# A final one-tile batch with pieces of its own, and one-tile exps in two parts

## The chip, the cores and the metric

The kernel runs on one core of one Trainium2 chip. The time is device microseconds of one execution. The kernel before took 336.56 us in the median of three runs (335.83 to 337.37). The execution that was profiled took 335.54 us, of which the span from the first to the last instruction is 333.7 us.

## The reference

32 sequences of at most 512 rows, each with its own length, go through multi-head self-attention with 8 heads of 64 columns. Rows past a sequence's length stay zero.

```
for b in range(batch):
    x_b = x[b, :lengths[b]]
    q, k, v = split(x_b @ w_qkv, 3)            # 512 -> 3 * 512
    q, k, v = [heads of 64 columns, (8, seq_len, 64)]
    scores = (q @ k.T) / sqrt(64)
    attn = exp(scores - max) ; attn /= sum(attn) + 1e-8
    output[b, :lengths[b]] = concat_heads(attn @ v)
```

The lengths are drawn between 64 and 511. In the draw used here the six shortest are 134, 119, 101, 86, 79 and 75.

## The kernel before

**Tiling.** The batches are ranked by length, longest first, and run in pairs (ranks 0 and 1, 2 and 3, and so on). The longer of the two sets the pair's class: a number of rows N from `CLASSES` (multiples of 32, and 340), with T = ceil(N / 128) tiles of 128 rows. In this draw the last pairs have 134 and 119 rows (class 160, two tiles), 101 and 86 (class 128, one tile), and 79 and 75 (class 96, one tile). For each class the program holds straight-line code for two halves, `h` = 0 and 1, one for each batch of a pair.

**A half is software-pipelined.** The half of batch r, with `g = 1 - h`, computes the attention of batch r, and the projections of batch r + 1 and their first scores. With one tile (`T == 1` in `half`, line 691) TensorE's order is: 16 products for the next batch's queries into bank `a0`, 16 for its keys into `a1`, 8 products of exps and values for this batch (`attnv`, line 548), 4 products for the next batch's values (`vwhole`, line 470), 8 score products for the next batch (`scores`, line 306 for the instruction, called at the end of `half`).

VectorE copies `a0` to `qkT` (line 412), takes the reciprocals of the eight sums (line 615), multiplies all eight heads with them and with the row mask in one instruction (line 640), and copies the values to `v_aug` (line 481). ScalarE copies `a1` (line 411), does the exps of all eight heads in one instruction (line 348), and issues the store of the batch (`act_store`, line 832; the DMA itself at line 844), for which it loads the batch's index first (line 1305). The exps are written to `ep`, the ninth element of each head in `v_aug` is the row mask, so that the product also gives the sums.

**Waits.** Each PSUM bank has a semaphore `full` (TensorE to the engine that empties it) and `free` (back). `acquire` makes TensorE wait until a bank is free; `close` puts the `full` on the last product of a group and hangs further signals (`pr.signals`) on the products before it. The exps' `free` is also what the product of exps and values waits for. The normalized output `onat[h]` is guarded by `s_of` (written) and `s_od` (stored).

**Blocks and branches.** `graph` (line 1155) lays the code of each class in blocks: `first` (half 0), then either `again` (half 1, when the next pair has the same class) or `last` (half 1, when it has another), then `tail`, which goes on to the next class. For classes of one tile the `again` blocks lie behind all classes, and `first` ends with a branch (line 1267) that goes on to `last` or away to `again`:

```
bye = name == "act" and T == 1
...
if T == 1:
    br = e.br_cmp(cur, k, out_, label(k, "again"), "IS_NE")
```

ScalarE alone has another block: `mid` (line 1275) looks whether any batch follows, and if none does it goes to `bye`, also behind all classes, where the store is issued ahead of the exp. TensorE and VectorE run the ordinary `last` block for the final batch too: they compute projections, values and scores of a batch that does not exist, from whatever the buffers hold.

**The end.** SyncE (queue SP) transposes, loads and stores for the longer batches; GpSimd (POOL) casts and places rows. After its loops SyncE waits for ScalarE's end (`s_fin`), for the landing of the last stores (line 1642), and then all engines meet in barriers.

Of the kernel before, what the change touches and what calls it, by code (L numbers as in the profile page):

```python
# [11 lines left out]
ALU = mybir.AluOpType  # L12
# [140 lines left out]
def kernel(  # L153
# [118 lines left out]
    for b in halves_av:  # L272
        for g in ("act", "dve"):
            full[(b, g)] = sem(f"f_{b}_{g}")
    free = {b: sem(f"e_{b}") for b in banks + halves_av + ("x0",)}
    area = {
        "a0": pa[:, 0], "a1": pa[:, 1],
        "v0": pav[:, 0:MAXS], "v1": pav[:, MAXS : 2 * MAXS],
# [29 lines left out]
    def scores(pr, slot, h, i, kts, T, N):  # L308

        b = f"s{slot}"  # L310
        qk_h = qkT[h]
        if T == 1:
            def po(par, i, kt):
                return psc[:, slot, par, P * i : P * i + N]

            items = [(j, 0) for j in range(NPAIR)]
            src = psc[:, slot].rearrange("p a (i n) -> p a i n", n=P)[:, :, :, 0:N]
            dst = ep[:, :, :, 0, 0:N].rearrange("p i a n -> p a i n")
        elif T == 2:
            def po(par, i, kt):  # L320
                return psc[:, slot, par, 256 * kt : 256 * kt + N]

            items = [(i, 0), (i, 1)]
            src = psc[:, slot].rearrange("p a (t n) -> p a t n", n=256)[:, :, :, 0:N]
            dst = ep[:, i, :, 0:2, 0:N]
        else:
            def po(par, i, kt):
                return psc[:, slot, par, 0:N]

            items = [(i, kts)]  # L330
            src = psc[:, slot, :, 0:N]
            dst = ep[:, i, :, kts, 0:N]
        mms = []
        for j, kt in items:
            for par in range(2):
                rq = HD * par
                mms.append(
                    mm(
                        po(par, j, kt),
                        qk_h[rq : rq + HD, 2 * j + 1, kt * P : (kt + 1) * P],  # L340
                        qk_h[rq : rq + HD, 2 * j, 0:N],
                        True,
                        True,
                    )
                )
        group(
            pr, b, "act", mms,
            lambda e: e.activation(out=dst, in_=src, func=AF.Exp, scale=scale),  # L348
        )
        pr.pair[b] = i  # L350

    def scores_dense(pr, h, i, N, T):
# [195 lines left out]
    def attnv(pr, h, i, T, late=False, b=None, qts=None):  # L548

        for s_ in ("s0", "s1"):  # L550
            if pr.pair[s_] == i or T == 1 and pr.pair[s_] is not None:
                acquire(pr, s_)
        for v in halves_av if b is None else (b,):
            acquire(pr, v)
        va = v_aug[h]
        if b is not None:
            jobs = [(2 * 74 * k, i, qt) for k, qt in enumerate(qts)]
        elif T == 1:
            jobs = [(74 * 2 * j, j, 0) for j in range(NPAIR)]
        elif T == 4:  # L560
            jobs = [(256 * qt, i, qt) for qt in range(T)]
        else:
            jobs = [(74 * (4 * qt + 2 * (i % 2)), i, qt) for qt in range(T)]
# [19 lines left out]
        if b is not None:  # L583
            n = len(qts)
            res = into[:, 0 : 2 * 74 * n].rearrange("p (t a d) -> p t a d", a=2, d=74)
            dst = on[:, i // 2, qts[0] : qts[0] + n, P * (i % 2) : P * (i % 2 + 1)]
            dst = dst.rearrange("p t (a d) -> p t a d", d=HD)
            sh, fin = [n, 2], i % 2 == 1 and T - 1 in qts
        elif T == 4:
            res = pav.rearrange("p (j n) -> p j n", n=256)[:, :, 0 : 2 * (HD + 1)]  # L590
            res = res.rearrange("p j (a d) -> p j a d", d=HD + 1)
            dst = on[:, i // 2, :, P * (i % 2) : P * (i % 2 + 1)]
            dst = dst.rearrange("p t (a d) -> p t a d", d=HD)
            sh, fin = [NT, 2], i % 2 == 1
        else:
            sh, fin = [2, 4] if T == 1 else [T, 4], True
            res = pav[:, 0 : 74 * sh[0] * 4].rearrange("p (b j d) -> p b j d", j=4, d=74)
            if T == 1:
                dst = on[:, :, 0, :].rearrange("p b (j d) -> p b j d", d=HD)
            else:  # L600
                dst = on[:, i // 2, 0:T, :].rearrange("p t (a d) -> p t a d", d=HD)
        r0 = 2 * qts[0] if b is not None else 0
        rv = rcp[:, i, r0 : r0 + sh[0] * sh[1]].rearrange("p (j a) -> p j a", a=sh[1])
        num, den = res[..., 0:HD], res[..., HD]
# [4 lines left out]

        def recip():  # L610
            opens = i % 2 == 0 and (b is None or 0 in qts)
            for j in (0, 1) if T == 1 else (i // 2,) if not each or opens else ():
                pr.take("dve", s_od[h][j], 16)
            pr.take("dve", full[(name, "dve")])
            pr.add("dve", lambda e: e.reciprocal(out=rv, in_=den).then_inc(s_r, 1))  # L615

        def mult():
            pr.take("dve", s_r)

            if T == 1:  # L620
                cuts = [(slice(0, 2), 0)]
            elif b is not None:
                whole = [] if h else [k for k, t in enumerate(qts) if t < T - 1]
                cuts = [(slice(0, len(whole)), None)] if whole else []
                cuts += [(slice(k, k + 1), t) for k, t in enumerate(qts) if k not in whole]
            elif h == 0:
                cuts = [(slice(0, T - 1), None), (slice(T - 1, T), T - 1)]
            else:
                cuts = [(slice(t, t + 1), t) for t in range(T)]

            def fn(e):
                for w, t in cuts:
                    ops = dict(
                        out=dst[:, w], in0=num[:, w],
                        in1=rv[:, w].unsqueeze(3).broadcast_to(list(num[:, w].shape)),
                    )
                    if t is None:
                        ins = e.tensor_tensor(op=ALU.mult, **ops)
                    else:
                        ins = e.scalar_tensor_tensor(  # L640
                            scalar=now[0][:, 1, t : t + 1], op0=ALU.mult, op1=ALU.mult, **ops
                        )
                if fin:
                    ins.then_inc(s_of[h][i // 2], 1)
                if back is not None:
                    if fin:
                        ins = e.memset(small, 0.0)
                    ins.then_inc(free[back], 1)

            pr.add("dve", fn)  # L650
            if back is not None:
                pr.busy[back] = True

        todo = {"R": recip, "X": mult}
        if not late:
            for fn in todo.values():
                fn()
        return todo

    def acquire_carry(pr, mms):  # L660
        carry, pr.signals = pr.signals, []
# [31 lines left out]
    def half(pr, h, T, N, W, st, last=False):  # L693
# [2 lines left out]
        tiles = -(-W // P)  # L696
        pr.signals += [s_vf[g]] if T == 1 else [s_xtf[h], s_vf[g]]

        def start_proj():
            if not st["x"]:  # L700
                st["x"] = True
                pr.take("pe", s_xt[g], 64)
                pr.signals.append(s_x16f[g])

        if T == 1:
            start_proj()
            qk(pr, "a0", g, [(i, 0) for i in range(NPAIR)], W, P)
            qk(pr, "a1", g, [(i, 1) for i in range(NPAIR)], W, P, "act")
            attnv(pr, h, 0, 1)
            vwhole(pr, g)  # L710
            read_class(pr, h)
            for b in ("a0", "a1"):
                acquire(pr, b)
            pr.signals.append(s_xtf[g])
            pr.take("pe", s_on[g])
            if last:
                act_store(pr, h, 0, T)
            scores(pr, h, g, 0, 0, 1, W)
            if not last:
                act_store(pr, h, 0, T)  # L720
            return
        per = T if T >= 3 else 1
        ahead = tiles if T >= 3 else 1
# [138 lines left out]
    def make_body(N, W, last=False):  # L862
# [4 lines left out]
        for h in range(2):  # L867
            st["x"] = False
            pr.add("dve", lambda e: set_now(e))
            half(pr, h, T, N, (N, W)[h], st, last and h == 1)  # L870
            pr.add("dve", lambda e: e.reg_add(rank_reg[0], rank_reg[0], 1))
            if h == 0:
                pr.second = {g: len(ops) for g, ops in pr.ops.items()}
        assert (st["slot"], st["bank"], len(st["banks"])) == (0, 0, len(area))
        ops = [op for op in pr.ops["pe"] if isinstance(op, Matmuls)]
        ops[-1].carry([free[b] for b in banks + halves_av if not pr.busy[b]])
# [281 lines left out]
    def graph(e, name, opening=None, before=None):  # L1158
# [86 lines left out]
        for k, N in enumerate(CLASSES):  # L1245
# [15 lines left out]
                stay[N].run_part(e, 0, cut(k) or stay[N].second[name], entry)  # L1261
            else:
                stay[N].run_half(name, e, 0)
            bye = name == "act" and T == 1
            out_ = label(k, "mid" if bye else "last")
            if T == 1:
                br = e.br_cmp(cur, k, out_, label(k, "again"), "IS_NE")
            else:
                br = e.br_cmp(cur, k, label(k, "again"), out_, "IS_EQ")
                again(k)  # L1270
# [19 lines left out]
        for k, N in enumerate(CLASSES):  # L1290
            if N <= P:
                again(k)
            if name == "act" and N <= P:
                open_(label(k, "bye"))
                final[N].run_half(name, e, 1)
                e.br(label(n, "end"))
# [578 lines left out]
```

## Time and profile before

| What | Value |
|---|---|
| median of three runs | 336.56 us |
| the profiled execution | 335.54 us |
| its span | 333.7 us |
| mean granted TensorE clock | 0.994 |
| TensorE products, busy | 321.6 us (96%) |
| ScalarE, busy | 247.0 us (74%) |
| VectorE, busy | 204.8 us (61%) |
| GpSimd, busy | 67.6 us (20%) |
| `ACT ep L348`, 193 exps | 157.0 us |
| `out_dram<-onat`, ACTq, 256 KB, 16 stores | 3.4 us to landing |

How to read it: busy time of an engine counts its instructions of work; branches, register and semaphore instructions and the issuing of DMAs are not in it. In a row of the timeline stand the start in microseconds from the span's start, the duration, the engine, the source line, the operation, what it writes and reads, its shape and count, and in brackets the idle time before it with what ended it. PE is a TensorE product, PEld its weight load, ACT is ScalarE, DVE VectorE, a trailing q means the engine's sequencer or queue. The four one-tile halves are the last 20 us of the span, out of 333.7; in the rest nothing of the code is touched.

### The profile page before, as it was taken

The page shows a single profiled execution, that of the slowest core. Times are in us where ns is not written, and L with a number is a line of the kernel's source. Part 1 is how long each engine was busy: PE and PEld are TensorE (multiplying, and loading weights), DVE is VectorE, ACT ScalarE, POOL GpSimd, SP SyncE. Part 2 cuts the span into 40 slices and gives each one's busy share as a digit, 9 for nine tenths or more (in the row PEclk, how much of TensorE's full clock was granted, in tenths as well). Part 3 has the DMA queues.
Part 4 walks back from the last instruction along what each step waited for, and adds up shares of the span by engine and source line. Part 5 has one row for each costly group of instructions (what it writes and reads, how often), then busy time and mean ns, then how long its engine had stood idle before and what let it go on. Part 6 is the DMA issues. An engine that isn't in the chain of part 4 may idle for free. (4 is left out here: it accounts for less than half of the span.)

```text
span 333.7 us, 12386 instructions
## 1 busy us (share of the span) xinstructions
PE 321.6 (96%) x4388; PEld 208.0 (62%) x4389; DVE 204.8 (61%) x578; ACT 247.0 (74%) x357; POOL 67.6 (20%) x126
## 2 busy tenths in 40 slices
PE   6999999999999999999999999999999999999991
PEld 2665544455565656566566666677677777787760
DVE  3676567556475575566566557665745656767671
ACT  4568787788889878878978887887677676666641
POOL 3634020201011210220220222022111231131340
PEclk9999999999999999999999999999999999999997
DMA  6976799956654986985787987998688667768742
GB/s 211 346 175 217 194 387 223 324 152 219 142 197 126 333 264 172 293 305 163 238 313 215 226 285 257 204 240 227 197 148 206 206 182 161 177 195 140 202 140 71
DMA packets 83234, 72.35 MB, mean 217 GB/s; under 512 B 41612, under 2 KB 64140, under 8 KB 83156
## 3 DMA queue, kind: packets, MB, share of 16 engines
q1 hardware_dynamic: 71300, 59.84, 65.7%
q10 hardware_dynamic: 11856, 11.54, 10.1%
q8 instruction: 40, 0.66, 0.8%
q14 instruction: 38, 0.31, 0.3%
HBM read 25.32 MB, written 36.70 MB: 186 GB/s over the span
## 5 line engine op out<-in xcount | busy, mean ns | idle before, releaser
L348 ACT ACTIVATE ep<-psc 128x704 f16<-128x704 f32 (+7 forms) x193 | 157.0, 860 | 45.0 <-PE psc L306 32.3
L306 PE MATMUL pa<-xT,w_r 128*128 128x224 f16 (+21 forms) x984 | 122.9, 276 | 1.5 <-DVE qkT L412 0.7
L306 PEld LDWEIGHTS pa<-xT,w_r 128*128 128x128 f16 (+1 forms) x984 | 71.8, 97 | 29.6 <-issue 8.8
L306 PE MATMUL psc<-qkT 64*128 64x352 f16 (+17 forms) x700 | 68.2, 287 | 0.8 <-ACT ep L380 0.2
L412 DVE CAST qkT<-pa 128x512 f16<-128x512 f32 (+9 forms) x61 | 35.0, 574 | 44.5 <-PE pa L306 40.5
L306 PE MATMUL pa<-w_r,xT 128*128 128x512 f16 (+4 forms) x332 | 57.9, 330 | 0.0
L306 PE MATMUL pav<-v_aug,ep 128*128 128x65 f16 x1254 | 55.0, 194 | 0.4 <-PEq L61 0.4
L306 PEld LDWEIGHTS pav<-v_aug,ep 128*128 128x128 f16 x1254 | 49.0, 98 | 9.2 <-issue 1.7
L306 PE MATMUL pav<-xT,w_r 64*128 64x352 f16 (+12 forms) x392 | 50.8, 307 | 0.0
L380 ACT ACTIVATE ep<-psc 128x960 f16<-128x960 f32 (+3 forms) x48 | 42.9, 952 | 9.1 <-PE psc L306 6.0
L411 ACT CAST qkT<-pa 128x320 f16<-128x320 f32 (+8 forms) x74 | 34.4, 470 | 18.8 <-PE pa L306 13.6
L640 DVE SCALAR_TENSOR_TENSOR onat<-pav,masks,rcp 128x128 f32<-128x128 f32 (+2 forms) x124 | 44.4, 396 | 5.0 <-DVE rcp L615 1.9
L1713 POOL MEMSET v_aug<- 128x256 f16 x24 | 7.5, 314 | 186.2 <-POOLq L1301 186.2
L306 PEld LDWEIGHTS psc<-qkT 64*128 64x128 f16 x700 | 26.5, 94 | 28.1 <-issue 17.6
L1707 POOL CAST x<-x_nat 128x1536 f16<-128x1536 f32 (+3 forms) x33 | 42.0, 1272 | 7.9 <-POOLq L1301 7.7
L435 DVE TENSOR_TENSOR v_aug<-pa,masks 128x512 f16<-128x512 f32 (+1 forms) x46 | 30.7, 673 | 16.7 <-PE pa L306 16.4
L306 PEld LDWEIGHTS pav<-xT,w_r 64*128 64x128 f16 (+1 forms) x392 | 26.6, 94 | 12.4 <-issue 1.3
L306 PEld LDWEIGHTS pa<-w_r,xT 128*128 128x128 f16 (+2 forms) x332 | 22.7, 98 | 16.6 <-issue 4.1
L306 PE MATMUL pav<-w_r,xT 128*128 128x512 f16 (+3 forms) x124 | 26.9, 350 | 0.0
L615 DVE RECIPROCAL rcp<-pav 128x8 f32<-128x8 f32 (+2 forms) x69 | 13.6, 197 | 19.7 <-PE pav L306 15.1
L306 PEld LDWEIGHTS pa<-v_aug,ep 128*128 128x128 f16 x538 | 19.7, 98 | 7.0 <-issue 2.9
L306 PE MATMUL pa<-v_aug,ep 128*128 128x65 f16 x538 | 22.3, 194 | 0.0
(84 smaller groups left out, 169.8 us busy)
## 6 DMA issues: line engine op xcount, KB each, us to landing
out_dram<-zt SPq DMA_DIRECT2D x16, 768.0 KB, 6.0
x_nat<-in_x_dram SPq DMA_DIRECT2D x12, 512.0 KB
x_nat<-in_x_dram SPq DMA_DIRECT2D x5, 1024.0 KB
out_dram<-onat ACTq DMA_DIRECT2D x12, 384.0 KB, 5.2
out_dram<-onat SPq DMA_DIRECT2D x12, 384.0 KB, 4.5
x_nat<-in_x_dram SPq DMA_DIRECT2D x17, 256.0 KB, 5.7
out_dram<-onat ACTq DMA_DIRECT2D x16, 256.0 KB, 3.4
x_nat<-in_x_dram SPq DMA_DIRECT2D x4, 768.0 KB
```

What stands on the lines that cost most here:

```text
L306: return lambda e: e.matmul(o, lhsT, rhs, start=start, stop=stop)
L348: lambda e: e.activation(out=dst, in_=src, func=AF.Exp, scale=scale),
L380: lambda e, par=par, b=b: e.activation(out=ep[:, i, par, 0:T, 0:N], in_=psc_f[:, par, 0 : T * N].rearrange("p (t n) -> p t n", n=N), func= ...
L411: return lambda e: e.copy(out=dst, in_=src)
L412: return lambda e: e.tensor_copy(out=dst, in_=src)
L435: return lambda e: e.tensor_tensor(out=v_aug[h][:, t, lo // HD : lo // HD + n, 0:HD], in0=area[b][:, 0:w].rearrange("p (a d) -> p a d", d=HD),
L615: pr.add("dve", lambda e: e.reciprocal(out=rv, in_=den).then_inc(s_r, 1))
L640: ins = e.scalar_tensor_tensor(scalar=now[0][:, 1, t : t + 1], op0=ALU.mult, op1=ALU.mult, **ops)
L1707: e.tensor_copy(out=x16[h][:, 0:T, :], in_=x_nat[h][:, 0:T, :]).then_inc(s_xc[h], 1)
L1713: e.memset(v_aug[h][:, T - 1, NPAIR:NH, 0:HD], 0.0)
```

## The change

Four things are changed, all for classes of one tile.

- **Exps in two parts.** `scores` no longer closes the group with one exp for eight heads but with two, of four heads each. The first raises a new semaphore `s_part`, the second the bank's `free`.
- **`attn_one` in place of `attnv`.** Of the eight products of exps and values, four wait for the first part and four for the second. In the ordinary half the normalization stays one reciprocal and one multiply over all heads.
- **The final batch's own pieces.** With `last`, `half` does nothing but the attention of this batch: no projections, values, scores or exps for a next one. The two groups of four heads go to two PSUM banks, with a reciprocal and a multiply each, and ScalarE stores each half of the columns with a DMA of its own (`store`, the form of line 1309 before, with one tile) instead of one DMA for both. The signals that release POOL and SP are hung on the first products.
- **The blocks.** TensorE and VectorE have `mid` and `bye` as ScalarE has. The branch at the end of `first` is now the same for all classes: `again` follows `first` directly, and `mid` and `last` lie behind it; `bye` lies behind all classes.

```diff
+    s_part = [sem(f"s_part{h}") for h in range(2)]
@@ scores
+            parts = [slice(0, 2), slice(2, NPAIR)]
...
-        group(
-            pr, b, "act", mms,
-            lambda e: e.activation(out=dst, in_=src, func=AF.Exp, scale=scale),
-        )
+        def exp(e, part=None):
+            at = (slice(None), slice(None), part) if part else slice(None)
+            return e.activation(out=dst[at], in_=src[at], func=AF.Exp, scale=scale)
+
+        if T == 1:
+            acquire(pr, b)
+            close(pr, b, "act", mms, False)
+            pr.take("act", full[(b, "act")])
+            pr.add("act", lambda e: exp(e, parts[0]).then_inc(s_part[slot], 1))
+            pr.add("act", lambda e: exp(e, parts[1]).then_inc(free[b], 1))
+            pr.busy[b] = True
+        else:
+            group(pr, b, "act", mms, exp)
@@ new
+    def attn_one(pr, h, ends):
+
+        for v in (f"s{h}",) + halves_av:
+            acquire(pr, v)
+        pr.take("pe", s_part[1 - h])
+        size = MAXS if ends else 74 * 4
+        res = pav[:, 0 : 2 * size].rearrange("p (b n) -> p b n", b=2)[:, :, 0 : 74 * 4]
+        res = res.rearrange("p b (j d) -> p b j d", d=74)[:, :, :, 0 : HD + 1]
+        mms = [
+            mm(res[:, k // 4, k % 4, :], ep[:, k // 2, k % 2, 0, 0:P], v_aug[h][:, 0, k, :],
+               True, True)
+            for k in range(NH)
+        ]
+        av = full[("av", "dve")]
+        if ends:
+            close(pr, "av", "dve", mms[:NPAIR], False)
+        else:
+            acquire_carry(pr, mms[:NPAIR])
+        acquire(pr, f"s{1 - h}")
+        close(pr, "av", "dve", mms[NPAIR:], False)
+        dst = onat[h][:, :, 0, :].rearrange("p b (j d) -> p b j d", d=HD)
+        rv = rcp[:, 0, 0:NH].rearrange("p (b j) -> p b j", j=4)
+        for j in range(2):
+            pr.take("dve", s_od[h][j], 16)
+
+        def recip(w):
+            pr.take("dve", av)
+            pr.add("dve", lambda e: e.reciprocal(out=rv[:, w], in_=res[:, w, :, HD]).then_inc(
+                s_r, 1))
+
+        def mult(w, done):
+            pr.take("dve", s_r)
+            num = res[:, w, :, 0:HD]
+            pr.add("dve", lambda e: e.scalar_tensor_tensor(
+                out=dst[:, w], in0=num, scalar=now[0][:, 1, 0:1],
+                in1=rv[:, w].unsqueeze(3).broadcast_to(list(num.shape)),
+                op0=ALU.mult, op1=ALU.mult,
+            ).then_inc(s_of[h][done], 1))
+
+        parts = (slice(0, 1), slice(1, 2)) if ends else (slice(0, 2),)
+        for w in parts:
+            recip(w)
+        for done, w in enumerate(parts):
+            mult(w, done)
@@ half
+        if last:
+            pr.signals += [s_x16f[g], s_xtf[g]]
+            attn_one(pr, h, True)
+            pr.add("act", act_index)
+            for j in range(2):
+                pr.take("act", s_of[h][j])
+                pr.add("act", lambda e, j=j: store(e, regs_act["bi"], h, j, T))
+            return
...
-            attnv(pr, h, 0, 1)
+            attn_one(pr, h, False)
...
-            if last:
-                act_store(pr, h, 0, T)
             scores(pr, h, g, 0, 0, 1, W)
-            if not last:
-                act_store(pr, h, 0, T)
+            act_store(pr, h, 0, T)
@@ graph
-            bye = name == "act" and T == 1
+            bye = T == 1
...
-                br = e.br_cmp(cur, k, out_, label(k, "again"), "IS_NE")
+                br = e.br_cmp(cur, k, label(k, "again"), out_, "IS_EQ")
...
-            if name == "act" and N <= P:
+            if N <= P:
                 open_(label(k, "bye"))
```

More of the change, by code (lines that the diff above doesn't have):

```diff
@@ L550, in attnv @@
         for s_ in ("s0", "s1"):
-            if pr.pair[s_] == i or T == 1 and pr.pair[s_] is not None:
+            if pr.pair[s_] == i:
                 acquire(pr, s_)
@@ L557, in attnv @@
             jobs = [(2 * 74 * k, i, qt) for k, qt in enumerate(qts)]
-        elif T == 1:
-            jobs = [(74 * 2 * j, j, 0) for j in range(NPAIR)]
         elif T == 4:
@@ L595, in attnv @@
         else:
-            sh, fin = [2, 4] if T == 1 else [T, 4], True
+            sh, fin = [T, 4], True
             res = pav[:, 0 : 74 * sh[0] * 4].rearrange("p (b j d) -> p b j d", j=4, d=74)
[L598 to L601, printed above, removed]
+            dst = on[:, i // 2, 0:T, :].rearrange("p t (a d) -> p t a d", d=HD)
         r0 = 2 * qts[0] if b is not None else 0
@@ L611, in recip @@
             opens = i % 2 == 0 and (b is None or 0 in qts)
-            for j in (0, 1) if T == 1 else (i // 2,) if not each or opens else ():
+            for j in (i // 2,) if not each or opens else ():
                 pr.take("dve", s_od[h][j], 16)
@@ L618, in mult @@
             pr.take("dve", s_r)
-            if T == 1:
-                cuts = [(slice(0, 2), 0)]
-            elif b is not None:
+            if b is not None:
                 whole = [] if h else [k for k, t in enumerate(qts) if t < T - 1]
@@ L873, in make_body @@
                 pr.second = {g: len(ops) for g, ops in pr.ops.items()}
+        if last:
+            return pr
         assert (st["slot"], st["bank"], len(st["banks"])) == (0, 0, len(area))
```

## The prediction

> **What bounds the kernel now.** The page's head and its chain of waits come first, because the chain tells which end of the kernel is being cut.
>
> ```profile
> span 333.7 us, 12386 instructions
> ACT ep L348 0%
> L1642 SPq EVENT_SEMAPHORE  x1: 2591/2591/2591, 328.5 to 328.5; - x1
> SPq L1642 <- DMA out_dram<-onat: 2.6, 1, 2.6
> ```
>
> The chain names only the last exp on ScalarE, which is a shred of the span: the work that really ends last does not show as busy time. The other two rows are of line 1642, SyncE's wait for the landed stores, and of SyncE's own waits: from 328.5 it waits 2.59 us for a store of `onat`, to 331.06, and the remaining 2.6 us of the span are the closing barriers. So the end is: last product, its normalization, its store, its landing. The timeline of the last two halves shows that path:
>
> ```profile
> 320.50 0.34 PE L306 MATMUL psc<-qkT 64*128 64x96 f16 x8
> 322.54 0.32 PEld L306 LDWEIGHTS pav<-v_aug,ep 128*128 128x128 f16 x8 [0.28 <-issue]
> 322.83 1.02 PE L306 MATMUL psc<-w_r,xT 128*128 128x512 f16 x4
> 323.78 0.34 PE L306 MATMUL psc<-qkT 64*128 64x96 f16 x8
> 324.06 1.11 PE L306 MATMUL pa<-xT,w_r 128*128 128x64 f16 x32
> 324.10 0.75 DVE L481 TENSOR_SCALAR v_aug<-psc,masks 128x512 f16<-128x512 f32 x1
> 324.27 0.81 ACT L348 ACTIVATE ep<-psc 128x768 f16<-128x768 f32 x1 [0.95 <-ACTq L61]
> 325.35 0.32 PEld L306 LDWEIGHTS pav<-v_aug,ep 128*128 128x128 f16 x8 [0.30 <-issue]
> 325.38 0.42 PE L306 MATMUL pav<-v_aug,ep 128*128 128x65 f16 x8 [0.21 <-PEq L61]
> 325.64 1.02 PE L306 MATMUL psc<-w_r,xT 128*128 128x512 f16 x4
> 325.95 0.21 DVE L615 RECIPROCAL rcp<-pav 128x8 f32<-128x8 f32 x1 [0.54 <-DVEq L61]
> 326.23 0.37 ACT L411 CAST qkT<-pa 128x256 f16<-128x256 f32 x1 [1.15 <-ACTq L61]
> 326.41 0.75 DVE L640 SCALAR_TENSOR_TENSOR onat<-pav,masks,rcp 128x512 f32<-128x512 f32 x1 [0.25 <-DVEq L61]
> 327.40 0.56 ACTq L844 DMA_DIRECT2D out_dram<-onat  x1
> 328.18 0.60 ACT L348 ACTIVATE ep<-psc 128x512 f16<-128x512 f32 x1 [1.58 <-ACTq L61]
> ```
>
> Read: exp 324.27 to 325.08, product 325.35 to 325.80, reciprocal 325.95 to 326.16, multiply 326.41 to 327.16, store issued at 327.40. The projections of 64 columns at 324.06, the value projection at 325.64 and the exp at 328.18 belong to a batch that does not exist. The projections end at 325.17 and the product cannot start until the exp's 325.08, so they cost the path nearly nothing.
>
> The last leg, 327.40 to 331.04, is the longest. The stores of line 844 (the first row pair without the final one, the second the final one alone), and the DMA queues in three stretches (328.1 to 328.6, 328.6 to 329.5, 329.55 to 331.1; the last column is a share of 16 engines over the stretch):
>
> ```profile
> L844 ACTq DMA_DIRECT2D out_dram<-onat x3: 556/557/688, 318.7 to 325.0; - x3
> DMA to landing us min/median/max: 2.5/2.5/2.6
> ...
> L844 ACTq DMA_DIRECT2D out_dram<-onat x1: 557/557/557, 327.4 to 327.4; - x1
> DMA to landing us min/median/max: 3.6/3.6/3.6
> ...
> q8 instruction: 1, 0.02, 16.9%
> q10 hardware_dynamic: 255, 0.25, 77.4%
> q10 hardware_dynamic: 16, 0.02, 4.2%
> ```
>
> Three equal stores landed in 2.5 us; the final one took 3.6. A packet of instructions starts before 328.6 and holds one DMA engine for 0.169 x 16 x 0.5 = 1.35 us; 255 of the store's 272 packets then move within 0.9 us, and 16 trickle out after 329.55. One engine's share of the store stood behind the instructions: about 1.1 us of the end.
>
> **Part 1: the final batch's own pieces.** Removed: 32 projections, 4 value projections, 8 scores on TensorE, two evacuations on VectorE, a cast and an exp on ScalarE, all of them beside or behind the path above: worth 0, except the cast that stands ahead of the final index load in ScalarE's order (about 0.1 us of waiting and dispatch). POOL's and SP's pieces for the missing batch stay; they are released by the product's first three matmuls instead of the projections, some 0.9 us later, and SP was idle from before 328.5, so that costs 0 with cover down to 329.
>
> What is added is a way there. The final pieces now lie in a block of their own behind the others on TensorE and VectorE as already on ScalarE, and the "mid" and "last" blocks lie behind the "again" block. The branch rows:
>
> ```profile
> L1269 PEldq COMPARE_BRANCH  x14: 66/340/367, 42.0 to 308.1; - x14
> L1269 DVEq COMPARE_BRANCH  x14: 43/63/63, 43.9 to 309.4; - x14
> L1228 PEldq COMPARE_BRANCH  x13: 75/86/528, 23.6 to 326.9; - x13
> L1267 PEldq COMPARE_BRANCH  x2: 66/66/66, 317.1 to 323.5; - x2
> L1267 DVEq COMPARE_BRANCH  x2: 43/43/43, 318.4 to 324.7; - x2
> L1275 ACTq COMPARE_BRANCH  x2: 34/42/50, 319.5 to 325.7; - x2
> ```
>
> Line 1267, this branch today, falls through in 66 ns on TensorE. Line 1269, the same branch of larger classes, jumps over an "again" block at 340 ns, and the dearest jump of the kernel, to the end, is 528. TensorE meets the branch at 323.5 and needs the final product's weights at about 324.9: 0.34 + 0.53 is covered, up to 1.4 us. VectorE meets it at 324.7 and needs its reciprocal at 325.5: its two jumps have no row; between 0.1 (two times 63 ns) and 1.0 (two of TensorE's dearest) I take 0.4, nearest to the VectorE rows, which is hidden. ScalarE makes its far jump today: branch at 325.7, next instruction by 326.23, half a microsecond; the nearer jump adds about 0.1.
>
> [...]
>
> **Part 2: exps in two parts, four halves.** By form:
>
> ```profile
> L348 ACT ACTIVATE ep<-psc x5: 597/810/1023, 314.6 to 328.2; 128x1024 f16<-128x1024 f32 x2, 128x768 f16<-128x768 f32 x2, 128x512 f16<-128x512 f32 x1
> 300.60 1.30 ACT L348 ACTIVATE ep<-psc 128x640 f16<-128x640 f32 x2
> ```
>
> 512, 768 and 1024 columns take 597, 810 and 1023 ns: 0.83 ns a column and 0.17 fixed. Two parts of 384 are 0.49 each; two neighbours of 640 took 0.65 each where the fit gives 0.70, so the pair is some 0.93: its end is 0.12 later than the whole, its first half 0.3 earlier. For the earlier three halves the product waits for projections, so the price is on TensorE: one wait more (the two waits ahead of 325.35 held it 0.27 after the exp, so 0.05 to 0.15 each), and one jump at 317.1 that grows from 66 to 340 ns. In the half at 322.54 the bubble of 0.28 is exposed already. I take +0.15 for the start of the last exp (bounds -0.1, the first four products going early, and +0.5, three waits at 0.15 bare).
>
> **Part 3: two halves of product, normalization and store.** From an exp at 324.42: second part done 325.35, its weights 0.2 later (bounds 0.1 and 0.27), four products instead of eight end at 325.87 (0.19 for one, three more at 0.03); before it was 325.80. The first four are through by then. Second reciprocal 0.15 later, as now, 326.02 to 326.23. The multiplies and the store's other form:
>
> ```profile
> L640 DVE SCALAR_TENSOR_TENSOR onat<-pav,masks,rcp x3: 475/484/751, 314.0 to 317.0; 128x256 f32<-128x256 f32 x2, 128x512 f32<-128x512 f32 x1
> L1309 ACTq DMA_DIRECT2D out_dram<-onat x1: 379/379/379, 314.1 to 314.1; - x1
> L1309 SPq DMA_DIRECT2D out_dram<-onat x1: 413/413/413, 318.0 to 318.0; - x1
> DMA to landing us min/median/max: 2.1/2.2/2.3
> L1305 ACTq TENSOR_LOAD <-idx x32: 274/287/689, 42.1 to 326.3; - x32
> ```
>
> Two multiplies at 0.48 follow without the 0.25 gap, since their waits are met: 326.75 and 327.2, against 327.16. ScalarE's index load begins at 326.3 today; with 0.15 from upstream, 0.1 for the nearer jump, 0.1 less for the cast and 0.5 for the load it is through at about 327.0, so the first store goes at 327.2; it takes 0.38 to issue, and with the 0.24 from data to issue seen today (327.16 to 327.40) the second goes at 327.8, 0.4 later than today's only one. Its bytes are half. A store of this form and 256 KB lands in 2.1 to 2.3; halving the 0.9 us of movement makes 1.85 (bounds 1.6 and 2.3). It lands at 329.65, against 331.04: about -1.4 us, and -1.3 after rounding the unseen VectorE jump in.
>
> [...]
>
> The gain is thus not in the arithmetic (0.1 either way) but in the landing: 1.1 because TensorE is done by 325.6 and fetches its closing instructions before the stores move, 0.4 for fewer bytes and 0.3 for the shorter issue form, less 0.4 for issuing in series.
>
> **The rivals.** First, the second store stands behind an instruction packet as the single one does: for it, that a packet followed each engine's late jumps and the change adds jumps; against, that these fall near 325 to 327 and the packets of the second store near 329. Price 1.1 to 1.35: 336.5, no change.
>
> [...]
>
> [...]
>
> Fourth, a larger gain: the final index load at its 0.29 and VectorE's first multiply at 326.5 let the stores go at 326.75 and 327.2, landing at 328.95: -2.1, 334.5.
>
> **How the numbers follow.** The profiled execution took 335.54, 1.02 under the median of 336.56; a shift of -1.3 makes it 334.2, and the median 335.3, which I predict. The forecast (gain 0.7 to 1.7) has 0.58, the larger gain 0.16, the first rival 0.12, the second 0.08, the third 0.06. Half a per cent, 1.7 us, is about what a measurement of this kernel can tell from no change: faster than that is most of the larger gain and the forecast's edge with the spread of the runs, 0.22; slower only the third, 0.05; between them 0.73. The range from 334.2 to 336.7 takes in the larger gain and the first rival.
>
> **What would show it.** Right: SyncE's wait at its landed-store line ends near 329.7; two stores on ScalarE's queue some 0.6 apart with landings under 2.3; two exps of about 0.49 in the last four halves; no 64-column projections at the end. Wrong: a landing over 3, a gap of over 1.4 on TensorE between the last scores and the first product, or scores of the last halves that start over 0.5 later than 320.50 and 323.78.

## The result, and the profile after

The changed kernel takes 338.77 us in the median of five runs (338.65 to 339.18), against 336.56 (335.83 to 337.37) before: a ratio of 1.0072, interval 1.005 to 1.0095. It is slower by about 2.2 us, where 335.3 was forecast.

The profiled execution after took 338.9 us with a span of 337.1, which is 3.4 more than the profiled one before. One microsecond of that is the choice of executions: before's was 1.02 under its median, after's 0.13 over its own. The two traces differ upstream by 1.8 us: the last scores start at 325.55 instead of 323.78, and 1.5 of it is there ahead of the first class, where TensorE's branch of line 1300 (1243 before) starts at 24.9 instead of 23.4. Within the last pair it loses nothing: its two groups of scores lie 3.25 us apart (322.30, 325.55) and lay 3.28 apart before (320.50, 323.78). What the change did is therefore read from the last scores on.

The timeline of the changed kernel from there:

```profile
322.30 0.35 PE L307 MATMUL psc<-qkT 64*128 64x96 f16 x8 [0.17 <-PEq L61]
...
325.55 0.34 PE L307 MATMUL psc<-qkT 64*128 64x96 f16 x8
...
326.04 0.87 ACT L350 ACTIVATE ep<-psc 128x384 f16<-128x384 f32 x2 [0.76 <-ACTq L61]
...
329.83 0.47 PEld L307 LDWEIGHTS pav<-v_aug,ep 128*128 128x128 f16 x8 [4.08 <-issue]
329.86 0.60 PE L307 MATMUL pav<-v_aug,ep 128*128 128x65 f16 x8 [3.96 <-PEq L61]
330.27 0.51 DVE L691 RECIPROCAL rcp<-pav 128x4 f32<-128x4 f32 x2 [3.65 <-PE pav L307]
330.75 0.88 DVE L697 SCALAR_TENSOR_TENSOR onat<-pav,masks,rcp 128x256 f32<-128x256 f32 x2
331.50 0.98 ACTq L1366 DMA_DIRECT2D out_dram<-onat  x2
```

The two exps end at 326.91 and the products start at 329.86. Nothing that they need is late: their weight load waited 4.08 us for "issue", and the reciprocal's 3.65 is only that wait passed on. What TensorE's sequencer did in it stands in its branches. The groups of three source lines (duration minimum/median/maximum, then the first and the last start) are line 1324, the branch at the end of `first`, line 1332, the one from `mid` to the final block, and line 1353, the jump from there to the end:

```profile
L1324 PEldq COMPARE_BRANCH  x2: 225/473/721, 318.9 to 325.4; - x2
L1332 PEldq COMPARE_BRANCH  x2: 68/1707/3346, 319.1 to 326.2; - x2
L1332 DVEq COMPARE_BRANCH  x2: 43/52/62, 320.3 to 326.7; - x2
L1332 ACTq COMPARE_BRANCH  x2: 40/42/45, 321.4 to 327.6; - x2
L1353 PEldq COMPARE_BRANCH  x1: 2927/2927/2927, 330.1 to 330.1; - x1
```

On TensorE one branch, the jump to the final block at 326.2, took 3346 ns. The same line fell through in 68 ns seven microseconds earlier, and costs VectorE and ScalarE 62 and 45 ns. In the middle of that jump the DMA queues of the stretch from 326.8 to 328.2 show one packet of instructions on q8:

```profile
q8 instruction: 1, 0.02, 5.6%
```

It holds one of 16 engines for 0.056 x 16 x 1.4 = 1.25 us. The jump is thus longer than its packet, which starts at 326.86 in the trace: about 0.7 us before it and 1.4 behind it.

Part of the loss comes back at the stores. First the groups of line 1366, the two stores, with the time from issue to landing, and of line 1699, where SyncE has waited for them:

```profile
L1366 ACTq DMA_DIRECT2D out_dram<-onat x2: 351/363/375, 331.5 to 332.1; - x2
...
DMA to landing us min/median/max: 1.7/2.2/2.6
L1699 SPq EVENT_SEMAPHORE  x1: 28/28/28, 334.7 to 334.7; - x1
```

Then the DMA queues between 333.1 and 334.0, and between 333.85 and 334.8 (queue, kind, packets, MB, share of 16 engines):

```profile
q8 instruction: 1, 0.02, 10.6%
q14 instruction: 2, 0.02, 7.9%
...
q10 hardware_dynamic: 9, 0.01, 2.5%
```

The first store landed in 1.7 us. The second took 2.6: packets of instructions (two of q14, one of q8) moved at the same time, and the store's last nine packets trickle out after 333.85. That these nine stood behind such a packet on one engine is a reading; the view does not name the engines.

The leg from the last scores to the landing in both traces (us):

| Leg | before | after | difference |
|---|---|---|---|
| last scores to first final product | 1.60 | 4.31 | +2.71 |
| first final product to the last store's issue | 2.02 | 2.26 | +0.24 |
| issue of the last store to its landing | 3.64 | 2.61 | -1.03 |
| sum | 7.26 | 9.18 | +1.92 |
| landing to the end of the span | 2.69 | 2.37 | -0.32 |

The net of +1.6 lies near the 2.2 of the medians; the other 0.6 I could not place. The +0.24 is partly the clock: the eight products took 0.60 us at a granted clock of 0.50 (it is 0.50 from 327.9 on), where they took 0.42 at 1.00 before. With the jump announced (below), at nearly the same wait (3.91 us against 3.96), they took 0.44, and the last slice of `PEclk` on that page is 6. In the changed kernel's page that slice is 5 where all others are 9:

```profile
PEclk9999999999999999999999999999999999999995
```

### The profile page after: what moved, and what is told of

Read it like the earlier page. It is cut to its first block, busy times and chain, and to the rows that moved or that the text cites. A ratio compares the mean times of both kernels' runs of the same rounds, so it can differ in the third digit from the quotient of the medians.

```text
span 337.1 us, 12292 instructions
## 1 busy us (share of the span) xinstructions
PE 321.3 (95%) x4344; PEld 207.7 (62%) x4345; DVE 204.7 (61%) x578; ACT 246.4 (73%) x359; POOL 67.4 (20%) x126
## 5 line engine op out<-in xcount | busy, mean ns | idle before, releaser
L350 ACT ACTIVATE ep<-psc 128x704 f16<-128x704 f32 (+8 forms) x196 | 156.8, 849 | 43.6 <-PE psc L307 32.9
L307 PE MATMUL pa<-xT,w_r 128*128 128x224 f16 (+19 forms) x952 | 121.7, 278 | 1.9 <-DVE qkT L1014 0.9
L307 PEld LDWEIGHTS pa<-xT,w_r 128*128 128x128 f16 (+1 forms) x952 | 70.9, 97 | 29.6 <-issue 8.9
L644 DVE SCALAR_TENSOR_TENSOR onat<-pav,masks,rcp 128x128 f32<-128x128 f32 (+1 forms) x120 | 41.4, 384 | 4.2 <-DVE rcp L621 1.6
L621 DVE RECIPROCAL rcp<-pav 128x8 f32<-128x8 f32 (+2 forms) x65 | 12.7, 196 | 17.5 <-PE pav L307 14.5
```

The lines of the kernel that those rows point to most:

```text
L307: return lambda e: e.matmul(o, lhsT, rhs, start=start, stop=stop)
L350: return e.activation(out=dst[at], in_=src[at], func=AF.Exp, scale=scale)
L644: ins = e.scalar_tensor_tensor(scalar=now[0][:, 1, t : t + 1], op0=ALU.mult, op1=ALU.mult, **ops)
```

## Experiments

Ratios are to the kernel before, measured on the same chip beside each set. The theory (A) is that TensorE's one jump to the far block costs 3 us (3346 ns in the trace) and is the whole loss, because its code is not yet fetched; that reason is an assumption, since the traces show packets of instructions but not what an engine holds. The rivals are the exps in parts, the two stores, and a block that costs its fetch wherever it lies (B in the last set).

**The final block directly behind its branch.** Only the order of the targets is turned, which lays the block of the first-named target behind the branch:

```diff
-                e.br_cmp(cur, n, label(k, "last"), label(k, "bye"), "IS_LT")
+                e.br_cmp(cur, n, label(k, "bye"), label(k, "last"), "IS_EQ")
```

> The changed kernel with one edit: the final block lies directly behind the branch that leads to it, on all engines, instead of behind all classes. Theory A (TensorE's branch to a block that lies far off held it for 3.35 us in the changed kernel's trace, and that is the loss): the branch at that line falls under 0.2 us, the idle time between the last scores and the final product falls from 4.1 us to about 0.9, and the time falls by some 2.7 us to 336 (335.3 to 336.7). Theory B (the loss is in the 1.5 us that the changed kernel's trace is late before the first loop, or in the two stores): the time stays at 338 or above.

Measured: 335.94 us, ratio 0.9959 (0.9935 to 0.9984), so 1.4 us under the kernel before. The groups of the branch, of the jump to the end and of the two stores:

```profile
L1332 PEldq COMPARE_BRANCH  x2: 63/145/227, 319.0 to 326.1; - x2
...
L1353 PEldq COMPARE_BRANCH  x1: 4326/4326/4326, 326.9 to 326.9; - x1
...
L1366 ACTq DMA_DIRECT2D out_dram<-onat x2: 527/853/1179, 328.3 to 329.1; - x2
...
DMA to landing us min/median/max: 3.1/3.3/3.5
```

Its timeline, last scores and first final products:

```profile
325.36 0.35 PE L307 MATMUL psc<-qkT 64*128 64x96 f16 x8
...
326.67 0.48 PE L307 MATMUL pav<-v_aug,ep 128*128 128x65 f16 x8 [0.96 <-PEq L61]
```

Its DMA queues from 326.5 to 332.5:

```profile
q8 instruction: 3, 0.05, 4.6%
q14 instruction: 4, 0.03, 2.1%
```

The 3.35 us are gone: 1.31 from the scores to the products. The dear jump has moved behind the products (line 1353, 4326 ns), where nobody waits for it, but packets of instructions (three of q8, four of q14) now move in the stretch of the stores: each takes 3.1 us or more to land, against 1.7 for the changed kernel's first. From the last scores to the last landing it is 6.77 us, against 7.26 before and 9.18 in the changed kernel.

**A far block for TensorE alone**, in the kernel before; the final batch runs its ordinary pieces there.

```diff
-            bye = name == "act" and T == 1
+            bye = name in ("act", "pe") and T == 1
...
-                final[N].run_half(name, e, 1)
+                (final if name == "act" else leave)[N].run_half(name, e, 1)
```

> The kernel before with one edit: TensorE alone reaches the final batch's unchanged pieces by a jump to a block behind all classes; nothing else is changed. Theory A: the branch takes about 3 us, of which 0.6 are covered by the scores in flight, and the time is 338.9 to 339.8. Theory B: the jump costs at most the 0.5 us of the dearest jump in the trace of before, and the time stays within 336 to 337.

Measured: 346.83 us, ratio 1.0302 (1.0255 to 1.0349): 10 us, three times what was expected. The groups of its branch to the block and of its last branch:

```profile
L1275 PEldq COMPARE_BRANCH  x2: 68/1789/3510, 320.2 to 327.2; - x2
...
L1870 PEldq COMPARE_BRANCH  x2: 179/1793/3407, 0.8 to 340.6; - x2
```

The timeline of its 32 projections in that block:

```profile
330.86 0.69 PE L306 MATMUL pa<-xT,w_r 128*128 128x64 f16 x10 [3.11 <-PEq L61]
333.84 1.35 PE L306 MATMUL pa<-xT,w_r 128*128 128x64 f16 x22 [2.29 <-issue]
```

The last branch of the kernel before, the same line:

```profile
L1870 PEldq COMPARE_BRANCH  x2: 179/242/306, 0.8 to 331.9; - x2
```

The jump alone (3510 ns), without the other parts, does the harm. The trace shows two more stops: the engine stops again after ten projections of the new block, for 2.3 us, and the branch at the very end takes 3407 ns where it took 306 before.

**The exps in two parts alone**: `scores` and `attn_one` of the changed kernel, the final batch as before.

```diff
-        group(pr, b, "act", mms, lambda e: e.activation(...))
+        if T == 1:
+            ...two exps of four heads, s_part and free
-            attnv(pr, h, 0, 1)
+            attn_one(pr, h, False)
```

> The exps in two parts and the product in two groups of four heads in all four one-tile halves, and nothing else: the final batch runs the ordinary block as before, with one store, and the blocks lie as before. Theory A: within 0.4 us of before, 336.2 to 337.0, since the scores of the last halves start no later. Theory B in the form that the parts cost: about 338.

Measured: 336.85 us, ratio 0.9995 (0.997 to 1.002). The parts neither gain nor cost.

**The block near, and the `again` blocks far**, as they were before the change:

```diff
-                br = e.br_cmp(cur, k, label(k, "again"), out_, "IS_EQ")
+                br = e.br_cmp(cur, k, out_, label(k, "again"), "IS_NE")
```

> The final block directly behind its branch, and the block for a further pair of the same class behind all classes again, as before the change, so that neither branch of the last pairs jumps. Theory A: TensorE's first branch falls from 0.72 to under 0.1 us too; the time is 335.0 to 336.3, 0.2 to 0.5 below the run with the near final block alone, and under the kernel before. Theory B: 338.

Measured: 339.3 us, ratio 1.0051 (1.0022 to 1.008); a miss. The stores land early, 5.87 us after the last scores instead of 7.26, but the program's last branch is on the path:

```profile
L1927 PEldq COMPARE_BRANCH  x2: 179/1974/3770, 0.8 to 331.6; - x2
```

It jumps over the `again` blocks after all stores have landed, in 3770 ns, and no work hides it. The kernel before has the same three blocks in the same place and pays 306 ns there. The length of the jump does not decide alone; what else does is not shown here.

**The jump announced.** In the changed kernel the outcome of the branch is announced in the entry of `first`, 3.4 us ahead:

```diff
+                if T == 1:
+                    end_hint.append(hint(cur, ALU.is_lt, n))
...
+                for at in end_hint:
+                    br.branch_hint(at)
```

> The changed kernel as it is, blocks where they are, with one instruction pair more on TensorE: behind the first 16 projections of a one-tile pair it announces whether the branch to the final block will be taken. Theory A (the branch waited for its instructions to be fetched): the branch falls from 3.35 us to under 0.6, the final product follows the last scores within 1.3 us, and the time is 335.0 to 336.3, 0.3 to 0.7% under the kernel before. Theory C (what counts is the position of the code and not the moment of the fetch): the branch stays at about 3 us and the time at 338.5.

Measured: 338.11 us, ratio 1.0015 (0.9989 to 1.0041). The groups of its branch and of its two stores:

```profile
L1336 PEldq COMPARE_BRANCH  x2: 68/1569/3070, 319.6 to 326.7; - x2
...
DMA to landing us min/median/max: 1.7/1.7/1.7
```

The branch still took 3070 ns, as theory C has it, and both pages count 41 packets on q8 and 38 on q14: with the announcement no packet more moved. The end is 1.1 us shorter than in the changed kernel (8.06 against 9.18 from scores to landing), 0.9 of it in the landing of the second store (1.7 against 2.6). Why the announcement did nothing is open; that the branch stands right behind another jump is a guess.

**The same announcement in the kernel with TensorE's far block alone.**

> The kernel before with TensorE's jump to the far block for the final batch, and with the same announcement. Its block holds 68 products, and in the run without announcement TensorE stopped a second time inside it, after 10 of them. Theory A: the branch falls from 3.5 us to under 0.6; the second stop either stays (then 342 to 344) or goes too (337 to 338). Theory C: 346 to 347 as without.

Measured: 345.82 us, ratio 1.0225 (1.0185 to 1.0265); the branch took 3630 ns. No help here either. Its 32 projections (the block holds 52 products, not 68) show the second stop again:

```profile
329.15 0.39 PE L306 MATMUL pa<-xT,w_r 128*128 128x64 f16 x8 [3.29 <-PEq L61]
332.44 1.44 PE L306 MATMUL pa<-xT,w_r 128*128 128x64 f16 x24 [2.89 <-issue]
```

It comes after eight products here and came after ten without the announcement, whose instructions push the block a little further on. So the stop seems to belong to a place in the code and not to a number of products.

**The exps whole again**, in the announced kernel (one exp of eight heads, all products behind it):

```diff
-        if T == 1:
-            ...two exps
-        else:
-            group(pr, b, "act", mms, exp)
+        group(pr, b, "act", mms, exp)
```

> As the first run of this set, but the exps of the four one-tile halves are one instruction each again and the eight products wait for it together; the final batch's two halves of normalization and store stay. If the parts are worth nothing (the first part's products wait for the second all the same): within 0.3 us of the first run. If the parts are what brings the final store forward: 0.3 to 0.6 us slower than it.

Measured: 337.6 us, ratio 0.9997 (0.9975 to 1.002), 0.5 us under the announced kernel with intervals that overlap. With the run of the parts alone: the parts are worth nothing that shows.

**One normalization and one store**, in the announced kernel:

```diff
-            attn_one(pr, h, True)
-            ...two stores
+            attn_one(pr, h, False)
+            act_store(pr, h, 0, T)
```

> As the first run of this set, but the final batch is normalized by one reciprocal and one multiply and stored by one DMA of 256 KB, in the form of before. The prediction had 0.4 us for fewer bytes, 0.3 for the shorter issue and minus 0.4 for issuing in series: by it this is 0.2 to 0.5 us slower than the first run, with a landing of about 2.5 us, or 3.6 if a packet of instructions stands ahead of it. If the two stores are no better than one: within 0.2 us, or faster.

Measured: 340.75 us, ratio 1.0095 (1.0062 to 1.0128), 2.6 us over the announced kernel. The group of its last store:

```profile
L896 ACTq DMA_DIRECT2D out_dram<-onat x1: 553/553/553, 331.7 to 331.7; - x1
...
DMA to landing us min/median/max: 2.8/2.8/2.8
```

From scores to landing it is 9.64 against 8.06 us: 1.1 of the 1.6 in the landing (2.8 against 1.7) and 0.35 in a longer gap at the jump of this trace (4.60 against 4.25), which is not the stores' doing. So in this place the two halves are worth more than was thought, about 1.2 us by the traces, though packets of instructions moved beside the one store too (three of q8 and three of q14 between 326 and 336). The medians differ by more; the execution that was profiled here is 2.0 under its median.

**The distance.** Four kernels in one set. The first, second and fourth leave out the class of 64 rows, which this draw never enters (its shortest pair has 79 and 75 rows): the changed kernel, the one with the block near, and the kernel before. In the first, 60 products of code then lie on TensorE between the branch and the final block, instead of 216. The third is the changed kernel with all classes and moves only the `again` block of class 64 behind everything: 164 products. (A half has 52 products and a final block 8; the expectations took a half for 60 and so say 68, 248 and 188. Their order is the same.)

```diff
-CLASSES = sorted([STEP * k for k in range(2, 17)] + [DENSE_ROWS], reverse=True)
+CLASSES = sorted([STEP * k for k in range(3, 17)] + [DENSE_ROWS], reverse=True)
```
```diff
+            if N == CLASSES[-1]:
+                br = e.br_cmp(cur, k, out_, label(k, "again"), "IS_NE")
+            elif T == 1:
```

> The changed kernel without its shortest class, 64 rows, which this draw never enters. On TensorE the code between the branch to the final block and that block shrinks from 248 products (the last half of class 96, three halves of class 64, one final block) to 68. Theory A, the price is one of distance (code not yet fetched): the branch takes 0.9 us or less instead of 3.35, the gap from the last scores to the first final product is 1.3 to 1.9 us, the time 335.3 to 336.6, ratio to the kernel before 0.994 to 0.999. Theory B, a block that was never run is paid for wherever it lies off the straight line: the branch again takes 3.0 to 3.6 us, the time is 338 to 339, ratio 1.002 to 1.007.

> The final block directly behind its branch, and no class of 64 rows. Both theories: the branch under 0.1 us, as with the block near and all classes; 335.2 to 336.4, ratio to the kernel before 0.993 to 0.998. The jump to the end is shorter now (68 products in place of 256): by theory A it falls from 4.3 us to under 1, its packets come before the stores, and these land in 2.3 us or less: 335.2. By theory B it stays over 3 us, hidden behind the stores.

> The changed kernel with one half of class 64 moved behind everything, so that 188 products instead of 248 lie between the branch and the final block. Theory A: a price between that of 248 products (3.35 us) and that of the 120 or so that the kernel before jumps over at its end (0.53 us); with fetches in packets of fixed size it is one or the other and not a value between. Theory B: 3.0 to 3.6 us. Time 335.3 to 336.6 if cheap; 338 to 339 if dear. The engine's last branch now passes 60 products, and shows a price for that distance also.

> The kernel before without its class of 64 rows: the control for what the missing class does by itself. Both theories: the final batch runs the ordinary half, the jump to the end is shorter (0.1 to 0.4 us instead of 0.53) and off the path; 336.4 to 337.4, ratio to the kernel before 0.997 to 1.003.

Measured: 334.69 us, ratio 0.9951 (0.9919 to 0.9983); 335.29, 0.9941 (0.9918 to 0.9963); 339.32, 1.0078 (1.0051 to 1.0105); and the control 335.73, 0.9965 (0.9941 to 0.9989). The groups of the branch, the stores and SyncE's wait of the first:

```profile
L1332 PEldq COMPARE_BRANCH  x2: 68/148/228, 318.1 to 325.6; - x2
...
L1366 ACTq DMA_DIRECT2D out_dram<-onat x2: 356/360/365, 327.9 to 328.5; - x2
...
DMA to landing us min/median/max: 1.7/1.7/1.7
L1699 SPq EVENT_SEMAPHORE  x1: 28/28/28, 330.3 to 330.3; - x1
```

Its timeline, last scores and first final products:

```profile
324.78 0.34 PE L307 MATMUL psc<-qkT 64*128 64x96 f16 x8
...
326.16 0.44 PE L307 MATMUL pav<-v_aug,ep 128*128 128x65 f16 x8 [1.03 <-PEq L61]
```

The group of the branch of the third:

```profile
L1334 PEldq COMPARE_BRANCH  x2: 68/1677/3286, 318.0 to 325.2; - x2
```

Rival B has fallen: the same block, never run before and off the straight line, costs 228 ns behind 60 products and 3286 behind 164. It is one or the other: between 164 and 216 products the price does not grow (3346). The packets of instructions, by which the expectation of the third kernel argues, hold 16 KB each on q8 (41 with 0.67 MB on the changed kernel's page) and 8 on q14 (38 with 0.31). In the second kernel the jump to the end took 181 ns and the stores landed in 1.9 and 2.1 us, as theory A has it. In the third, the jump to the end passes one final block of eight products, as it does in the changed kernel, where it took 2927 ns:

```profile
L1355 PEldq COMPARE_BRANCH  x1: 187/187/187, 329.0 to 329.0; - x1
```

So distance alone is not the measure. That where the code lies decides fits this and the moved second stop above, but no run varies it alone. The same kernel's last branch, over the one block moved behind, took 367 ns.

The control is a miss: leaving a class out that is not used was to change nothing, and gained 0.35%. Its final store shows where:

```profile
L844 ACTq DMA_DIRECT2D out_dram<-onat x1: 563/563/563, 331.4 to 331.4; - x1
DMA to landing us min/median/max: 2.4/2.4/2.4
```

It landed in 2.4 us where the kernel before took 3.6, and from the last scores to the landing it is 6.09 us against 7.26. That is about the 1.2 us between the medians, but it is read from one trace of each, and the control's profiled execution lay 2.8 above its median. Why the store lands sooner behind the shorter code is open. Against that control the changed kernel with the cheap jump is only 1.0 us faster (334.69 against 335.73), and the intervals overlap.

## Why the prediction was wrong

**The step that failed** is in part 1: TensorE's two jumps, "0.34 + 0.53 is covered, up to 1.4 us". They took 0.72 and 3.35 us, and the final products came 2.71 us later after the last scores than before. Moving nothing but that block (first experiment, 63 ns) turns a loss of 2.2 us into a gain of 1.4. That this is the forecast's size is luck: the stores landed in over 3 us there, where 1.85 was forecast, and the leg from scores to landing is only 0.5 under before's.

The prices were taken from rows of lines 1269 and 1228, and these are not short jumps. Two of them, each with the row of line 1188 that belongs to it:

```profile
L1188 PEldq BRANCH_PREFETCH_HINT  x1: 49/49/49, 26.1 to 26.1; - x1
L1269 PEldq COMPARE_BRANCH  x1: 367/367/367, 42.0 to 42.0; - x1
L1188 PEldq BRANCH_PREFETCH_HINT  x1: 40/40/40, 45.3 to 45.3; - x1
L1228 PEldq COMPARE_BRANCH  x1: 350/350/350, 61.1 to 61.1; - x1
```

By the code, the jump at 42.0 passes the `again` block of class 512, 208 products, and the one at 61.1 all of class 480, 624 products: about as far as the new jump's 216, and much further. What they have and the new branch has not is an announcement (line 1188), here 16 us ahead. The 528 ns jump, over 104 products, has one too, 2.6 us ahead (324.3 to 326.9). The branch at the end of `first` now has the same order for all classes, but only the larger ones announce it. So the rows priced announced jumps, and were applied to one that is not announced. Whether the announcement is what makes them cheap no run shows: none takes it away from a larger class, and the run that gave it to the new branch, 3.4 us ahead, changed nothing.

No run shows the prices per jump behind the chances of the second rival (0.08) and the third (0.06, and the 0.05 for slower). What the runs showed in their place: in the changed kernel TensorE's two branches to `mid` took 225 ns (at 318.9, under the scores' cover) and 721, and the one to the final block 3346, of which the packet took 1.25 us and 1.4 lay behind it; no jump of VectorE or ScalarE there took more than 63 ns.

**The first rival came true**, to 0.9 us: the second store met instruction packets and landed in 2.61, against 1.7 for the first and the forecast 1.85. The argument that the packets would be over by then fell with the late jumps. In the kernel where neither happened, the first of the distance set, the second store landed in 1.7 us, 5.5 us after the last scores (330.25 against 324.78), close to the forecast's 5.72 (329.65 less 323.93) and under before's 7.26.

**What held.** The exps took 0.87 a pair (0.93 forecast) and cost nothing upstream (0.15 forecast; the two scores groups stayed 3.25 apart, and the experiment with the parts alone gave 0.9995). The multiplies followed each other in 0.88 us without a gap. VectorE's and ScalarE's jumps took 62 and 45 ns and were hidden. The two stores were issued 0.63 apart (0.6 forecast), each in 0.35 to 0.38.

**What was argued only.** That the removed pieces were worth nothing on the path is plausible, but no run removes them alone. That 1.1 us of the gain comes from TensorE fetching its closing instructions earlier was the author's estimate, and no run shows it: the stores of 128 KB took 1.7 to 3.5 us over these kernels, and the control had that gain (2.4 against 3.6 us) with none of the new pieces.

## What to carry to other kernels

A block of its own for a rare case can cost more than its instructions: here TensorE's jump to it took 3346 ns over 216 products and 63 with the block directly behind its branch, so lay it there. Price a jump by a row that is like it in all that the code shows, distance and announcement both, or leave it unpriced with its full range. When cheap rows are to price a new jump, see first what they had that it has not: here an announcement, in the two rows above 16 us ahead.

## What the runs showed of the hardware

- TensorE's jump to the far block, over 164 to 216 products, took 3.1 to 3.6 us (3070 to 3630 ns in seven kernels), with an instruction packet of 1.25 us inside the one that was taken apart. Over 60 products it took 0.2 us (228 ns), and the branch to a block directly behind it 63 to 66 ns in three kernels.
- Length alone does not say which: a jump to the end over the same eight products took 2927 ns in the changed kernel and 187 in the third of the distance set; the same three blocks behind the program's end cost 306 ns before, and 3770 ns in the fourth experiment; and an announced jump over 624 products took 350 ns.
- Behind such a jump a second stop followed inside the new block in two kernels (2.3 us after ten projections in one, 2.9 after eight in the other).
- A store of 128 KB landed in 1.7 us in four kernels (the first of the two in the changed kernel, both in the announced one and in the first of the distance set, one in the third). With packets of instructions in the same stretch it took 2.6 us (one of q8 and two of q14, changed kernel) and 3.1 and 3.5 (three and four, block near). In the first of the distance set one packet of q14 moved between 327 and 331, and both stores landed in 1.7 us.
